# FFN of a hybrid decoder layer: squares, weight sums and sums for the residual moved between ScalarE, VectorE, GpSimd and PSUM

## The chip, the cores and the metric

The kernel runs on 1 core of one Trainium2 chip. The metric is the device time of one execution in microseconds (us); lower is better. Engines: PE is TensorE, DVE is VectorE, ACT is ScalarE, POOL is GpSimd, SP is SyncE, which issues the loads and stores of the stage in question.

## What is computed

The reference is one decoder layer: RMS norm, an RWKV-7 branch and a dilated attention branch with gates, a memory cross-attention, a squared-ReLU MLP (FFN) and a final RMS norm, on 1024 tokens of 1024 channels in fp32. The change lies in the FFN alone, which runs from 1719.5 us to the end:

```python
# D_MODEL = 1024, SEQ = 1024, FFN_DIM = 4096
u = rmsnorm(h, norm_ffn_g[l]) @ ffn_w1[l]
h = h + (jnp.square(jax.nn.relu(u)) @ ffn_w2[l]).astype(h.dtype)
return rmsnorm(h, norm_final_g)
```

## The kernel before

The FFN multiplies two by two blocks of matrices with seven block products in place of eight. There are 16 **up items** (p = 0 to 15, two 128-column tiles of `ffn_w1` each, both halves of the tokens) and then 4 **groups** of 4 **down items** (g, q: a quarter of the 4096 hidden channels, two tiles of the output). An item has seven **products** j = 0 to 6. A product (`seventh`) sums 4 blocks of 128 channels, and each block takes three matmuls of 128x512, high by high, high by low and low by high part (`L1422` to `L1424`), so it has 12 matmuls, and its sum stays in one of 4 PSUM tiles `ms`. After a product, `up_evac` or `down_evac` takes it off PSUM.

- **Weights** (`weights`): four quarters a0 to a3 (tile `sr`, 6 buffers, 256 KB each) are loaded from HBM on SP's queue. Sums c3 (`L1401`), c2 (`L1402`), c4 (`L1407`) and c6 (`L1410`) of them are formed on DVE in SBUF tiles `ws`. Each of the seven operands is split (`f_split`) into a high part `wh` (ACT, `L1384`) and a low part `wl` (POOL, `L1385`).
- **Moving operands** `com[j]`: four pairs (`ah`, `al`; for one j called `u`) for each j. The up items share one set that `first_coms` makes during the first 50 us of the stage, when the items p = 0 to 2 (the prologue) run products in the order in which it delivers them. For each group of down items `second` makes a new set of 28 pairs: the tile `ur` is read back from a DRAM scratch (`uscr`; 6 `ur` buffers), ACT casts it to `ah` (`L1534`), ACT copies `ah` to a PSUM tile `acc` (`L1536`), and DVE subtracts that from `ur` to give `al` (`L1537`). One pair in four goes without the PSUM copy (`L128`, `L129`).
- **up_evac** sums products into u11, u12, u21 and u22, squares each after ReLU with one DVE instruction (`squared`, `L1429`), forms t1 (`L1488`), t2 (`L1489`), the new u12 (`L1490`) and t4 (`L1491`) on DVE in SBUF, and stores seven tiles to `uscr`.
- **down_evac** adds the products to the residual `h` (SBUF). It keeps a running sum t (tile `sg`, SBUF). For j = 0 it is an ACT copy of the product (`L1503`), for j = 2 and j = 4 a DVE add (`sg<-sg,ms`). t is added to one h tile by DVE for j = 0, by POOL for j = 2, and to one by POOL and one by DVE for j = 4 (`h<-h,sg`). The other sums take a product straight from PSUM (`h<-h,ms`). All adds stand on `L1432`.

Products run in the order item:0, previous:5, item:1, previous:6, item:2, 3, 4, and the scheduler may interleave neighbours matmul by matmul. So a group's first item reads its new operands right after the previous item's j = 4, and 24 matmuls of previous:5 and previous:6 lie among them. The scheduler fixes each engine's order of instructions; each engine then runs strictly in that order and waits for semaphores. The pool behind `acc` has two buffers, handed out in program order: a tile of it can only be written when the tile two before it has been read for the last time. The pool behind `f` (`fps`) has two PSUM buffers too and is used by the norms at the FFN's start and end.

Of the kernel before, what the change touches and what calls it, by code (L numbers as in the profile page):

```python
# [41 lines left out]
def hybrid_layer(ctx, tc, x, mem, norm_mix_g, w_in, shift_mu, w0, w2, a0, a2, g2, k_k, k_a, r_k, gn_w, gn_b,  # L42
# [1336 lines left out]
    def f_split(raw):  # L1379
# [5 lines left out]
        nc.gpsimd.tensor_tensor(l, raw, h.bitcast(F32), op=ALU.subtract)  # L1385
# [5 lines left out]
    def weights(views, early=False):  # L1391
# [4 lines left out]
        def get(j):  # L1396
            if j < 2:
                return f_split(f_raw(views[j]) if early else a[j])
            if not c:
                c[3], c[2] = f_sum(), f_sum()  # L1400
                nc.vector.tensor_tensor(c[3], a[2], a[3], op=ALU.add)  # L1401
                nc.vector.tensor_tensor(c[2], c[3], a[0], op=ALU.subtract)  # L1402
            if j in (2, 3):
                return f_split(c[j])
            if j == 4:
                c[4] = f_sum()
                nc.vector.tensor_tensor(c[4], a[0], a[2], op=ALU.subtract)  # L1407
# [20 lines left out]
    def squared(dst, src):  # L1428
        nc.vector.scalar_tensor_tensor(dst, src, 0.0, src, op0=ALU.max, op1=ALU.mult)  # L1429

    def add(dst, a, b, eng=None):
        (eng or nc.vector).tensor_tensor(dst, a, b, op=ALU.add)  # L1432

    def up_evac(p, st, j):
# [8 lines left out]
        elif j == 1:  # L1443
            st["11"] = staged() if p >= PRO else bt.tile([P, H2], F32, tag="nt", name=nm("ua"))
            add(st["11"], st["a"], ps)
            if p >= PRO:
                squared(st["11"], st["11"])
            else:
                nc.scalar.activation(st["11"], st["11"], AF.Relu)
                nc.scalar.activation(st["11"], st["11"], AF.Square)  # L1450
# [29 lines left out]
        elif j == 6:  # L1480
# [5 lines left out]
            squared(u12, u12)  # L1486
            t1, t2, t4 = [staged() for _ in range(3)]
            nc.vector.tensor_tensor(t1, u12, u11, op=ALU.subtract)  # L1488
            nc.vector.tensor_tensor(t2, u22, t1, op=ALU.subtract)  # L1489
            nc.vector.tensor_tensor(u12, u22, u12, op=ALU.subtract)  # L1490
            nc.vector.tensor_tensor(t4, u21, t2, op=ALU.subtract)  # L1491
# [5 lines left out]
    def down_evac(g, q, st, j):  # L1497
        (h11, h12), (h21, h22) = [[hT[2 * q + e][half] for half in range(2)] for e in range(2)]
        ps = st["p", j]
        if j in (0, 2, 4):  # L1500
            t = staged()
            if j == 0:
                nc.scalar.copy(t, ps)  # L1503
            else:
                add(t, st["t"], ps)
            st["t"] = t
        if j == 0:
            add(h11, h11, t, nc.vector)
        elif j == 1:
            add(h11, h11, ps)  # L1510
        elif j == 2:
            add(h12, h12, t, nc.gpsimd)
        if j == 4:
            add(h21, h21, t, nc.gpsimd)
            add(h22, h22, t, nc.vector)
# [107 lines left out]
    def item(views, evac, **kw):  # L1623
        return dict(st={}, w=weights(views), evac=evac, **kw)

    def up_item(p):
        return item(up_views(p), lambda st, j: up_evac(p, st, j))
# [112 lines left out]
```

## Time and profile before

| | us |
|---|---|
| median of 3 runs (lowest to highest) | 2409.03 (2401.53 to 2418.07) |
| profiled execution | 2407.52 |
| its span | 2405.8 |
| PE busy in the span | 2292.9 (95%) |
| DVE / ACT / POOL busy | 1545.9 / 1088.3 / 889.4 |

The profiled execution's time is 1.7 us longer than its span. A matmul's busy time is longer than the pace at which matmuls follow each other, since they overlap; so PE's loss in a stretch is read as the stretch's length less the number of its matmuls times the undisturbed pace. In rows of the trace a line number such as L1422 is that of the kernel before, "x" counts instructions, and the last bracket gives the idle time of the engine before the row and what ended it.

### The profile page before, as it was taken

The page shows a single profiled execution, that of the slowest core. Times are in us where ns is not written, and L with a number is a line of the kernel's source. Part 1 is how long each engine was busy: PE and PEld are TensorE (multiplying, and loading weights), DVE is VectorE, ACT ScalarE, POOL GpSimd, SP SyncE. Part 2 cuts the span into 40 slices and gives each one's busy share as a digit, 9 for nine tenths or more (in the row PEclk, how much of TensorE's full clock was granted, in tenths as well). Part 3 has the DMA queues.
Part 4 walks back from the last instruction along what each step waited for, and adds up shares of the span by engine and source line. Part 5 has one row for each costly group of instructions (what it writes and reads, how often), then busy time and mean ns, then how long its engine had stood idle before and what let it go on. Part 6 is the DMA issues. An engine that isn't in the chain of part 4 may idle for free. (4 is left out here: it accounts for less than half of the span.)

```text
span 2405.8 us, 47020 instructions
## 1 busy us (share of the span) xinstructions
PE 2292.9 (95%) x18645; PEld 1827.2 (76%) x18645; DVE 1545.9 (64%) x2735; ACT 1088.3 (45%) x2118; POOL 889.4 (37%) x737
## 2 busy tenths in 40 slices
PE   6999999999999999999999999999989999899997
PEld 5777777777777777777777888888768888678785
DVE  6638676786776722233474666345799898876685
ACT  5525645546455434333443445444432222565464
POOL 4321222222222223111245534423535554566664
PEclk9999999999999999999999999999999999999998
DMA  5221111111111123121245554223244444653352
GB/s 174 58 65 35 37 39 35 37 42 28 34 38 37 46 67 106 41 67 45 82 149 161 168 150 135 81 61 87 81 133 152 149 145 160 217 167 118 119 156 71
DMA packets 301619, 226.73 MB, mean 94 GB/s; under 512 B 16229, under 2 KB 252375, under 8 KB 301399
## 3 DMA queue, kind: packets, MB, share of 16 engines
q1 hardware_dynamic: 301111, 223.20, 30.6%
q8 instruction: 147, 2.41, 0.4%
q14 instruction: 73, 0.60, 0.1%
q10 hardware_dynamic: 288, 0.52, 0.1%
HBM read 169.99 MB, written 53.67 MB: 93 GB/s over the span
## 5 line engine op out<-in xcount | busy, mean ns | idle before, releaser
L143 PE MATMUL acc<-ah,wh 128*128 128x512 f32 (+1 forms) x1600 | 652.4, 408 | 8.4 <-DVE al L1266 2.9
L144 PE MATMUL acc<-al,wh 128*128 128x512 f32 (+1 forms) x1600 | 618.2, 386 | 2.8 <-POOL al L231 1.5
L145 PE MATMUL acc<-ah,wl 128*128 128x512 f32 (+1 forms) x1600 | 618.2, 386 | 0.4 <-POOL wl L112 0.4
L112 POOL TENSOR_TENSOR wl<-wr,wh 128x512 fp32r<-128x512 f32 x248 | 334.6, 1350 | 706.9 <-ACT wh L110 668.3
L143 PEld LDWEIGHTS acc<-ah,wh 128*128 128x128 f32 x1600 | 302.8, 189 | 76.3 <-issue 3.9
L145 PEld LDWEIGHTS acc<-ah,wl 128*128 128x128 f32 x1600 | 302.7, 189 | 62.5 <-POOL wl L112 1.0
L144 PEld LDWEIGHTS acc<-al,wh 128*128 128x128 f32 x1600 | 303.4, 190 | 50.9 <-POOL al L231 3.3
L110 ACT CAST wh<-wr 128x512 fp32r<-128x512 f32 (+1 forms) x296 | 179.6, 607 | 299.2 <-PE acc L144 186.1
L1423 PE MATMUL ms<-al,wh 128*128 128x512 f32 x768 | 304.5, 396 | 10.4 <-DVE al L1537 5.4
L1422 PE MATMUL ms<-ah,wh 128*128 128x512 f32 x768 | 304.4, 397 | 5.4 <-ACT ah L128 2.5
L1424 PE MATMUL ms<-ah,wl 128*128 128x512 f32 x768 | 302.3, 394 | 0.0
L1385 POOL TENSOR_TENSOR wl<-ws,wh 128x512 fp32r<-128x512 f32 x128 | 178.6, 1398 | 177.7 <-ACT wh L1384 149.6
L1385 POOL TENSOR_TENSOR wl<-sr,wh 128x512 fp32r<-128x512 f32 x96 | 140.4, 1465 | 113.7 <-ACT wh L1384 113.6
L1423 PEld LDWEIGHTS ms<-al,wh 128*128 128x128 f32 x768 | 145.2, 189 | 48.7 <-DVE al L129 9.5
L1422 PEld LDWEIGHTS ms<-ah,wh 128*128 128x128 f32 x768 | 145.1, 189 | 41.9 <-ACT ah L128 5.0
L1424 PEld LDWEIGHTS ms<-ah,wl 128*128 128x128 f32 x768 | 145.2, 189 | 31.9 <-POOL wl L1385 0.2
L1384 ACT CAST wh<-ws 128x512 fp32r<-128x512 f32 x128 | 79.0, 620 | 171.5 <-PE ms L1423 145.9
L1384 ACT CAST wh<-sr 128x512 fp32r<-128x512 f32 x96 | 59.5, 620 | 147.7 <-PE ms L1423 136.7
L937 DVE CUSTOM_DVE_ANT_0 sS<-pS,bias 128x128 f32<-128x128 f32 (+1 forms) x96 | 30.2, 349 | 113.5 <-PE pS L125 113.3
L399 ACT ACTIVATE gt<-acc 128x512 f32<-128x512 f32 x32 | 19.0, 594 | 127.1 <-PE acc L145 121.3
L942 ACT ACTIVATE sS<-sS,nm 128x128 f32<-128x128 f32 (+1 forms) x96 | 42.5, 443 | 75.2 <-DVE nm L940 72.1
L1432 DVE TENSOR_TENSOR sg<-sg,ms 128x512 f32<-128x512 f32 x70 | 47.7, 683 | 37.5 <-PE ms L1424 36.6
(420 smaller groups left out, 4048.3 us busy)
## 6 DMA issues: line engine op xcount, KB each, us to landing
sr<-in_ffn_w_dram SPq DMA_DIRECT2D x134, 256.0 KB
wr<-in_w_in_dram SPq DMA_DIRECT2D x120, 256.0 KB
ur<-uscr SPq DMA_DIRECT2D x112, 256.0 KB
uscr<-sg SPq DMA_DIRECT2D x93, 256.0 KB
gtscr<-gt SPq DMA_DIRECT2D x32, 256.0 KB
g<-gtscr SPq DMA_DIRECT2D x32, 256.0 KB
wr<-in_p_rwkv_dram SPq DMA_DIRECT2D x32, 256.0 KB
wr<-in_w_out_dram SPq DMA_DIRECT2D x32, 256.0 KB
```

Of the source, the lines that this page charges most:

```text
L110: nc.scalar.copy(h, raw)
L112: lo_eng.tensor_tensor(l, raw, h.bitcast(F32), op=ALU.subtract)
L143: mms.append(nc.tensor.matmul(ps, h, ah, start=(k == 0), stop=False))
L144: mms.append(nc.tensor.matmul(ps, h, al, start=False, stop=False))
L145: mms.append(nc.tensor.matmul(ps, l, ah, start=False, stop=(k == len(acts) - 1)))
L942: nc.scalar.activation(sS[:, h, lo:], sS[:, h, lo:], AF.Exp, bias=nm2[:, h:h + 1], scale=0.125, accum_out=Og[:, b, 130 + h:131 + h])
L1384: nc.scalar.copy(h, raw)
L1385: nc.gpsimd.tensor_tensor(l, raw, h.bitcast(F32), op=ALU.subtract)
L1422: nc.tensor.matmul(ps, h[:, k, :], ah, start=(k == 0), stop=False)
L1423: nc.tensor.matmul(ps, h[:, k, :], al, start=False, stop=False)
L1424: nc.tensor.matmul(ps, l[:, k, :], ah, start=False, stop=(k == 3))
L1432: (eng or nc.vector).tensor_tensor(dst, a, b, op=ALU.add)
```

## The change

1. `squared` takes two ACT instructions (Relu in place, then Square) in place of one on DVE. Item p < 3 did so for u11 already.
2. In `up_evac` j = 6, the square of u12 goes to a PSUM tile b12 (`acc`), t2 is formed in a second one, b2, and ACT copies it from there to SBUF; three of the four subtractions read PSUM.
3. For up items from p = 3 and for the down items of groups 0 to 2, c3 and c2 are formed in the two `f` tiles in PSUM (named `wf`), and their low parts are split by DVE in place of POOL. c4 is a3 - c2 in place of a0 - a2 (the same value).
4. In `down_evac`, j = 0 adds the product itself to h11. For j = 2, t is formed in SBUF, ACT copies it to an `acc` tile b, and DVE adds b to h12 (POOL did). For j = 4 the sum goes to an `acc` tile b alone, and DVE adds it to h21 (POOL did) and h22.

In instructions of the whole program, DVE goes from 2670 to 2691, ACT from 1769 to 1926 and POOL from 724 to 642; PE (10971) and SP (905) keep theirs.

```diff
--- before.py
+++ after.py
@@ -1376,19 +1376,22 @@
         nc.sync.dma_start(t, ap)
         return t
 
-    def f_split(raw):
+    def f_split(raw, lo_eng=None):
         pool = wq[0] if wn[0] % 4 == 3 else wp
         wn[0] += 1
         h = pool.tile([P, 4, P], F32R, tag="wh", name=nm("wh"))
         l = pool.tile([P, 4, P], F32R, tag="wl", name=nm("wl"))
         nc.scalar.copy(h, raw)
-        nc.gpsimd.tensor_tensor(l, raw, h.bitcast(F32), op=ALU.subtract)
+        (lo_eng or nc.gpsimd).tensor_tensor(l, raw, h.bitcast(F32), op=ALU.subtract)
         return h, l
 
     def f_sum():
         return wrp[-1].tile([P, 4, P], F32, tag="wr", name=nm("ws"))
 
-    def weights(views, early=False):
+    def f_psum():
+        return fps.tile([P, 4, P], F32, tag="f", name=nm("wf"))
+
+    def weights(views, early=False, bank=False):
 
         a = [None if early else f_raw(v) for v in views]
         c = {}
@@ -1397,14 +1400,15 @@
             if j < 2:
                 return f_split(f_raw(views[j]) if early else a[j])
             if not c:
-                c[3], c[2] = f_sum(), f_sum()
+                c[3], c[2] = [f_psum() if bank else f_sum() for _ in range(2)]
                 nc.vector.tensor_tensor(c[3], a[2], a[3], op=ALU.add)
                 nc.vector.tensor_tensor(c[2], c[3], a[0], op=ALU.subtract)
             if j in (2, 3):
-                return f_split(c[j])
+                return f_split(c[j], nc.vector if bank else None)
             if j == 4:
+
                 c[4] = f_sum()
-                nc.vector.tensor_tensor(c[4], a[0], a[2], op=ALU.subtract)
+                nc.vector.tensor_tensor(c[4], a[3], c[2], op=ALU.subtract)
                 w = f_split(c[4])
                 c[6] = f_sum()
                 nc.vector.tensor_tensor(c[6], a[1], c[2], op=ALU.subtract)
@@ -1426,10 +1430,11 @@
                 yield
 
     def squared(dst, src):
-        nc.vector.scalar_tensor_tensor(dst, src, 0.0, src, op0=ALU.max, op1=ALU.mult)
-
-    def add(dst, a, b, eng=None):
-        (eng or nc.vector).tensor_tensor(dst, a, b, op=ALU.add)
+        nc.scalar.activation(src, src, AF.Relu)
+        nc.scalar.activation(dst, src, AF.Square)
+
+    def add(dst, a, b):
+        nc.vector.tensor_tensor(dst, a, b, op=ALU.add)
 
     def up_evac(p, st, j):
         def put(jj, t):
@@ -1443,11 +1448,7 @@
         elif j == 1:
             st["11"] = staged() if p >= PRO else bt.tile([P, H2], F32, tag="nt", name=nm("ua"))
             add(st["11"], st["a"], ps)
-            if p >= PRO:
-                squared(st["11"], st["11"])
-            else:
-                nc.scalar.activation(st["11"], st["11"], AF.Relu)
-                nc.scalar.activation(st["11"], st["11"], AF.Square)
+            squared(st["11"], st["11"])
             put(0, st["11"])
         elif p < PRO and j in (2, 3, 4):
 
@@ -1483,12 +1484,15 @@
                 nc.sync.dma_start(st["11"], uscr[p * 7 * P:(p * 7 + 1) * P, :])
             u11, u12, u21, u22 = st["11"], st["a"], st["21"], st["22"]
             add(u12, u12, ps)
-            squared(u12, u12)
+
+            b12, b2 = acc_tile(), acc_tile()
+            squared(b12, u12)
             t1, t2, t4 = [staged() for _ in range(3)]
-            nc.vector.tensor_tensor(t1, u12, u11, op=ALU.subtract)
-            nc.vector.tensor_tensor(t2, u22, t1, op=ALU.subtract)
-            nc.vector.tensor_tensor(u12, u22, u12, op=ALU.subtract)
-            nc.vector.tensor_tensor(t4, u21, t2, op=ALU.subtract)
+            nc.vector.tensor_tensor(t1, b12, u11, op=ALU.subtract)
+            nc.vector.tensor_tensor(u12, u22, b12, op=ALU.subtract)
+            nc.vector.tensor_tensor(b2, u22, t1, op=ALU.subtract)
+            nc.scalar.copy(t2, b2)
+            nc.vector.tensor_tensor(t4, u21, b2, op=ALU.subtract)
             put(3, t1)
             put(2, t2)
             put(4, u12)
@@ -1497,22 +1501,25 @@
     def down_evac(g, q, st, j):
         (h11, h12), (h21, h22) = [[hT[2 * q + e][half] for half in range(2)] for e in range(2)]
         ps = st["p", j]
-        if j in (0, 2, 4):
-            t = staged()
-            if j == 0:
-                nc.scalar.copy(t, ps)
-            else:
-                add(t, st["t"], ps)
-            st["t"] = t
         if j == 0:
-            add(h11, h11, t, nc.vector)
+            st["t"] = staged()
+            nc.scalar.copy(st["t"], ps)
+            add(h11, h11, ps)
         elif j == 1:
             add(h11, h11, ps)
         elif j == 2:
-            add(h12, h12, t, nc.gpsimd)
-        if j == 4:
-            add(h21, h21, t, nc.gpsimd)
-            add(h22, h22, t, nc.vector)
+
+            t = staged()
+            add(t, st["t"], ps)
+            st["t"] = t
+            b = acc_tile()
+            nc.scalar.copy(b, t)
+            add(h12, h12, b)
+        elif j == 4:
+            b = acc_tile()
+            add(b, st["t"], ps)
+            add(h21, h21, b)
+            add(h22, h22, b)
         if 3 in st["seen"] and 4 in st["seen"] and j in (3, 4):
             add(h22, h22, st["p", 3])
             add(h12, h12, st["p", 3])
@@ -1620,11 +1627,11 @@
         it["evac"](it["st"], j)
         yield
 
-    def item(views, evac, **kw):
-        return dict(st={}, w=weights(views), evac=evac, **kw)
+    def item(views, evac, bank=False, **kw):
+        return dict(st={}, w=weights(views, bank=bank), evac=evac, **kw)
 
     def up_item(p):
-        return item(up_views(p), lambda st, j: up_evac(p, st, j))
+        return item(up_views(p), lambda st, j: up_evac(p, st, j), True)
 
     PRO = 3
     early = []
@@ -1685,7 +1692,7 @@
                         gf.append(staged())
                         nc.scalar.dma_start(gf[e], norm_final_g[e * H2:(e + 1) * H2].rearrange("(o d) -> o d", o=1)
                                             .broadcast_to([P, H2]))
-                yield item(down_views(g, q), lambda st, j, g=g, q=q: down_evac(g, q, st, j), **kw), True
+                yield item(down_views(g, q), lambda st, j, g=g, q=q: down_evac(g, q, st, j), g < 3, **kw), True
 
     def stream():
         prev, ready = None, []
```

**VectorE at the last item of the prologue's first three, j = 6.** `ua`, `sg` with `ms` are sums of products; the row that PE's next product waits for is the first `sg<-ua,ms`. Before:

```order
L1432 TENSOR_TENSOR sg_19030<-sg_19030,ms_19150 128x512
L1402 TENSOR_TENSOR ws_19308<-ws_19307,sr_19247 128x512
L1429 SCALAR_TENSOR_TENSOR sg_19030<-sg_19030 128x512
L1407 TENSOR_TENSOR ws_19330<-sr_19247,sr_19251 128x512
L1488 TENSOR_TENSOR sg_19167<-sg_19030,sg_19163 128x512
L1410 TENSOR_TENSOR ws_19336<-sr_19249,ws_19308 128x512
L1489 TENSOR_TENSOR sg_19168<-sg_19061,sg_19167 128x512
L1490 TENSOR_TENSOR sg_19030<-sg_19061,sg_19030 128x512
L1491 TENSOR_TENSOR sg_19169<-ua_18785,sg_19168 128x512
L1432 TENSOR_TENSOR sg_19199<-ua_18886,ms_19186 128x512
```

After, where the add is L1437, c4 L1411 and the four subtractions L1491, L1492, L1493 and L1495:

```order
L1437 TENSOR_TENSOR sg_19030<-sg_19030,ms_19152 128x512
L1411 TENSOR_TENSOR ws_19342<-sr_19260,ws_19320 128x512
L1491 TENSOR_TENSOR sg_19172<-acc_19168,sg_19165 128x512
L1492 TENSOR_TENSOR sg_19030<-sg_19061,acc_19168 128x512
L1493 TENSOR_TENSOR acc_19169<-sg_19061,sg_19172 128x512
L1414 TENSOR_TENSOR ws_19348<-sr_19256,ws_19320 128x512
L1404 TENSOR_TENSOR wf_19495<-sr_19393,sr_19395 128x512
L1495 TENSOR_TENSOR sg_19174<-ua_18785,acc_19169 128x512
L1437 TENSOR_TENSOR sg_19205<-ua_18886,ms_19192 128x512
```

The square (`L1429`) is gone from VectorE and c2 (`L1402`) has moved ahead of the stretch; `L1491`, the first of the four subtractions, reads what ScalarE writes into `acc`, and c6 (`L1414` now) stands behind three of them.

**VectorE at the turn from group 0 to group 1.** Here `al` is a low part of the new group, `sg_22300<-` and `sg_22341<-` (before), `sg_22415<-` and `acc_22458<-` (after) are the running sums of the old group's last item for j = 2 and j = 4. Before:

```order
L1537 TENSOR_TENSOR al_22490<-ur_22497,acc_22500 128x512
L1432 TENSOR_TENSOR sg_22300<-sg_22222,ms_22287 128x512
L1537 TENSOR_TENSOR al_22492<-ur_22503,acc_22506 128x512
L1537 TENSOR_TENSOR al_22494<-ur_22509,acc_22512 128x512
L129 TENSOR_TENSOR al_22496<-ur_22515,ah_22495 128x512
L1537 TENSOR_TENSOR al_22544<-ur_22551,acc_22554 128x512
L1432 TENSOR_TENSOR sg_22341<-sg_22300,ms_22328 128x512
L1537 TENSOR_TENSOR al_22546<-ur_22557,acc_22560 128x512
L1432 TENSOR_TENSOR h_1_11297<-h_1_11297,sg_22341 128x512
L1537 TENSOR_TENSOR al_22548<-ur_22563,acc_22566 128x512
```

After:

```order
L1437 TENSOR_TENSOR sg_22415<-sg_22337,ms_22402 128x512
L1437 TENSOR_TENSOR h_1_11295<-h_1_11295,acc_22417 128x512
L1437 TENSOR_TENSOR acc_22458<-sg_22415,ms_22445 128x512
L1437 TENSOR_TENSOR h_0_11296<-h_0_11296,acc_22458 128x512
L1437 TENSOR_TENSOR h_1_11297<-h_1_11297,acc_22458 128x512
L1544 TENSOR_TENSOR al_22473<-ur_22480,acc_22483 128x512
L1437 TENSOR_TENSOR h_1_11297<-h_1_11297,ms_22424 128x512
L1437 TENSOR_TENSOR h_1_11295<-h_1_11295,ms_22424 128x512
L1544 TENSOR_TENSOR al_22475<-ur_22486,acc_22489 128x512
L1544 TENSOR_TENSOR al_22477<-ur_22492,acc_22495 128x512
```

Before, splits of the new group stand ahead of the sum for j = 2 and between it and the one for j = 4; after, the first split that goes through `acc` (and the first of all, since the others stand behind it) follows the three adds of j = 4.

**ScalarE at the same turn, after.** `wh` are weight casts, `acc_22417<-` is the copy of the running sum of j = 2, `acc_22483<-` the first copy of a new high part:

```order
L1541 CAST ah_22540<-ur_22548 128x512
L1541 CAST ah_22542<-ur_22554 128x512
L1384 CAST wh_22439<-ws_22437 128x512
L1384 CAST wh_22502<-sr_22464 128x512
L1384 CAST wh_22522<-sr_22318 128x512
L1516 COPY acc_22417<-sg_22415 128x512
L1384 CAST wh_22570<-sr_22466 128x512
L1384 CAST wh_22588<-ws_22443 128x512
L1543 COPY acc_22483<-ah_22472 128x512
```

Casts to `ah` run ahead of that copy as far as `ur` tiles are there, and no copy to `acc` does. In the new order of TensorE, counted in matmuls from the end of that j = 4, the low part of the 4th pair is first read by the 27th matmul, of the 8th by the 48th, of the 12th by the 60th, of the 16th by the 77th, of the 20th by the 90th, of the 24th by the 124th and of the 28th by the 135th.

**ScalarE at the last up item, j = 6, after.** `ua_21480` is its u12, `acc_21773` its t2 in PSUM, `ah` and `acc_21799` belong to the first down group:

```order
L1433 ACTIVATE ua_21480<-ua_21480 128x512
L1541 CAST ah_21844<-ur_21852 128x512
L1434 ACTIVATE acc_21772<-ua_21480 128x512
L1543 COPY acc_21799<-ah_21788 128x512
L1494 COPY sg_21777<-acc_21773 128x512
L1543 COPY acc_21805<-ah_21790 128x512
L1543 COPY acc_21811<-ah_21792 128x512
```

Its square and the copy of t2 stand between the copies of the first group's high parts; before, the low parts `al` of VectorE stood among the subtractions `L1488` to `L1491` of this item and were not tied to them through `acc`.

## Rows read from the trace of the kernel before

**Rows 1.** The page's head: span, busy time and share of each engine.

```profile
span 2405.8 us, 47020 instructions
PE 2292.9 (95%) x18645; PEld 1827.2 (76%) x18645; DVE 1545.9 (64%) x2735; ACT 1088.3 (45%) x2118; POOL 889.4 (37%) x737
```

**Rows 2.** Timeline of PE: start, duration, line; three matmuls on from the first row.

```profile
1731.18 0.39 PE L1422 MATMUL ms<-ah,wh 128*128 128x512 f32 x1
...
1731.86 0.39 PE L1422 MATMUL ms<-ah,wh 128*128 128x512 f32 x1
```

**Rows 3.** Windows: length; PE, PEld, DVE, ACT, POOL busy (x); clock; DMA; GB/s.

```profile
1720.00:1790.00 70.00, 58.17 (x225) 42.58 (x224) 66.30 (x99) 29.80 (x53) 23.57 (x18) 0.93 0.35 109
1900.00:1920.00 20.00, 20.00 (x88) 16.31 (x87) 18.33 (x20) 4.84 (x8) 10.45 (x8) 1.00 0.46 150
2040.00:2090.00 50.00, 41.67 (x167) 29.94 (x166) 44.74 (x65) 35.22 (x65) 23.95 (x17) 1.00 0.74 234
2140.00:2166.00 26.00, 23.86 (x102) 18.58 (x101) 21.46 (x28) 18.19 (x34) 15.30 (x12) 1.00 0.67 218
2220.00:2251.00 31.00, 28.45 (x114) 22.05 (x114) 24.98 (x34) 18.64 (x34) 18.35 (x13) 0.94 0.61 194
2300.00:2326.00 26.00, 25.36 (x111) 20.40 (x110) 23.42 (x32) 18.95 (x35) 17.53 (x13) 1.00 0.63 195
```

**Rows 4.** VectorE's instruction groups, 1715 to 2387 us: busy us, mean ns | idle before.

```profile
L1432 DVE TENSOR_TENSOR h<-h,ms 128x512 f32<-128x512 f32 x79 | 52.2, 677 | 4.4 <-PE ms L1424 4.4
L1407 DVE TENSOR_TENSOR ws<-sr,sr 128x512 f32<-128x512 f32 x32 | 47.1, 1472 | 2.4 <-POOL wl L1385 2.4
L1429 DVE SCALAR_TENSOR_TENSOR sg<-sg 128x512 f32<-128x512 f32 x45 | 45.3, 1008 | 0.9
L1432 DVE TENSOR_TENSOR h<-h,sg 128x512 f32<-128x512 f32 x32 | 34.6, 1084 | 8.3 <-ACT sg L1503 7.9
```

**Rows 5.** ScalarE's instruction groups of the same stretch.

```profile
L1536 ACT COPY acc<-ah 128x512 f32<-128x512 f32 x76 | 43.9, 586 | 7.3 <-DVE al L1537 4.3 <-issue 1.8 <-ACT ah L1534 0.3
L1534 ACT CAST ah<-ur 128x512 fp32r<-128x512 f32 x72 | 43.3, 618 | 22.0 <-DMA ur<-uscr 20.5 <-PE ms L1424 1.1
L1449 ACT ACTIVATE ua<-ua 128x512 f32<-128x512 f32 x3 | 1.9, 632 | 0.0
```

**Rows 6.** GpSimd's instruction groups of the same stretch.

```profile
L1385 POOL TENSOR_TENSOR wl<-ws,wh 128x512 fp32r<-128x512 f32 x128 | 178.6, 1398 | 177.7 <-ACT wh L1384 149.6 <-PE ms L1424 10.7 <-PE ms L1423 7.2
L1432 POOL TENSOR_TENSOR h<-h,sg 128x512 f32<-128x512 f32 x32 | 47.2, 1476 | 14.1 <-DVE sg L1432 8.8 <-PE ms L1424 5.4
```

**Rows 7.** Timeline of VectorE in the prologue, ten rows from u12's sum on.

```profile
1770.91 0.69 DVE L1432 TENSOR_TENSOR sg<-sg,ms 128x512 f32<-128x512 f32 x1 [0.18 <-PE ms L1424]
...
1773.14 1.77 DVE L1429 SCALAR_TENSOR_TENSOR sg<-sg 128x512 f32<-128x512 f32 x1
...
1780.61 0.68 DVE L1432 TENSOR_TENSOR sg<-ua,ms 128x512 f32<-128x512 f32 x1
```

**Rows 8.** Timeline of PE at the same place.

```profile
1781.43 0.47 PE L1422 MATMUL ms<-u,wh 128*128 128x512 f32 x1 [3.42 <-DVE sg L1432]
```

**Rows 9.** The splits' own work (tile ur): length, DVE busy (x), ACT busy (x), clock, DMA.

```profile
2115.00:2135.40 20.40, 10.18 (x13) 8.47 (x15) 1.00 0.53 155
2135.40:2162.00 26.60, 10.83 (x16) 8.26 (x14) 1.00 0.71 230
```

**Rows 10.** Timeline of VectorE at the turn to group 2.

```profile
2242.59 1.76 DVE L1407 TENSOR_TENSOR ws<-sr,sr 128x512 f32<-128x512 f32 x1 [1.19 <-POOL wl L1385]
2244.28 1.27 DVE L1432 TENSOR_TENSOR h<-h,ms 128x512 f32<-128x512 f32 x2
```

**Rows 11.** Timeline of GpSimd at the same place.

```profile
2242.52 1.28 POOL L1432 TENSOR_TENSOR h<-h,sg 128x512 f32<-128x512 f32 x1
```

**Rows 12.** Timeline of PE at the same place.

```profile
2245.69 0.47 PE L1422 MATMUL ms<-u,wh 128*128 128x512 f32 x1 [2.22 <-DVE h L1432]
...
2247.19 0.63 PE L1422 MATMUL ms<-u,wh 128*128 128x512 f32 x1
```

## The prediction

> **What bounds the kernel now.** I read the head of the page first, then windows along the FFN with PE's timeline beside them, then the costs of single instructions, then the places where PE waits. PE is busy for 95% of the span, so the span is PE's work plus what PE loses [rows 1]. The change leaves PE's 10971 instructions alone; only its losses can move. Three matmuls start in 1731.86 - 1731.18 = 0.68 us, 0.2275 us apart [rows 2]. A stretch of n matmuls therefore loses its length less 0.2275 n. With that the windows give, in order [rows 3]:
>
> - prologue, 1720 to 1790: 70 - 225 x 0.2275 = 18.8 us lost;
> - a steady stretch (1900 to 1920): 20 - 88 x 0.2275 = 0, with DVE at 18.3, ACT at 4.8 and POOL at 10.5 of 20 us;
> - up to down, 2040 to 2090: 50 - 167 x 0.2275 = 12.0 us lost, with DVE at 89% and the DMA engines at 0.74;
> - the three turns between groups: 26 - 102 x 0.2275 = 2.8, 31 - 114 x 0.2275 = 5.1, 26 - 111 x 0.2275 = 0.7, together 8.6 us.
>
> So some 39 us of PE time are at stake in the FFN, and no more than that can be won before its end. PE's loss is where DVE or ACT delivers an operand late; the share of busy time says nothing on that.
>
> **The steady stretch: 0.** An up item is 84 matmuls, 19.1 us. DVE loses four squares of 1008 ns [rows 4] and gets two low parts, each with one PSUM operand; the nearest row with one PSUM operand is `h<-h,ms`, 677 ns, and above it POOL's price of 1398 ns bounds it [rows 4, 6]. DVE comes down by 4.0 - 1.4 = 2.6 us. ACT gets four pairs of Relu (632 ns) and Square, for which I take the same, and a copy of 586 [rows 5], 5.6 us: from 4.8 to about 10.5 of 20. POOL gives up 2 x 1.4 = 2.8 us. No engine passes PE's 19.1, and PE waits for none of them in this stretch already; the cover is the distance between a product and its use. If that cover were gone, the price would be the longer square alone, 1.26 - 1.01 = 0.25 us x 4 an item, 13 items: 13 us. I see nothing that takes it away and count 0. c4 in its new form has one operand in PSUM: between 677 and 1472 ns [rows 4], not on PE's path here.
>
> A rule of the Trainium skill speaks against the squares: "ScalarE: Activation LUTs", Rules for kernel authors, wants relu, max and mul on VectorE, not on ScalarE. The rows agree on the sign (1008 ns against twice 632), but the engine that gets the longer work is idle for three quarters of this stretch, so by the rule the sum would move only where PE waits for ACT.
>
> **Prologue: -1.5 (bounds -6 to +2).** The largest wait is 3.42 us [rows 8], and it ends with DVE's `sg<-ua,ms` of 1780.61, ten instructions behind u12's sum of 1770.91 [rows 7]. Among them are c2, which now stands ahead, and the square of 1.77 us. On the other side ACT's Relu and Square, 1.26 us, must now come before the first subtraction, with only c4 beside them. Walked by hand from 1771.6: c4 hidden, square done 1773.0, three subtractions at 0.68 to 0.9, c6, one c3, the last subtraction, and the sum starts at about 1778.3 in place of 1780.6. That is 2.3 us, and a little of the half-clock matmuls behind the wait. Against it, earlier in the prologue ACT now also squares u22 of the first item, and in its new order that stands ahead of casts to `ah`: two instructions of 0.63 us [rows 5], of which I count 0.8 as lost (up to 1.8 with the half-clock matmuls). Net -1.5; the lower end is all of the 3.42 and its slow matmuls, the upper end the squares with no gain.
>
> **Up to down: -1 (-4 to +6).** 28 splits are made here, and 28 at each turn. Here item 15's squares leave DVE, which is at 89%, and that is worth up to three squares, 3 us. But its b12 and b2 now take both `acc` buffers in the middle of the first group's splits: the next split's copy waits for the four subtractions, and ACT stands with it. Before, splits were mixed with those subtractions. Walking the new order with the durations of [rows 4, 5], PE waits some 5 to 6 us for the first product after item 15's chain, 3 for the next that reads new splits, and 2 after that: 10 to 12 us in place of 12.0. The price if it goes wrong is one wait for a whole chain of squares and subtractions, 1.3 + 3 x 0.7 + 0.6 = 4 us, and a half more for the copy of t in the group's first item behind it.
>
> **Turns between groups: +8.5 (-5 to +38).** This is the term that decides. Before, DVE had made 13 of the new group's splits in the 20 us ahead of the running sum of j = 4 (2135.4), and 16 in the 26.6 us after it [rows 9]; together 1.62 us a split, unhurried. After, the copy of j = 2's t and the sum of j = 4 take both `acc` buffers, and 21 of 28 splits need `acc`; in DVE's new order the first of all stands behind the adds of j = 4. So nothing is ready when that product ends. PE has 24 matmuls of the old item to fill in (5.5 us).
>
> Let the first split end 2.6 us later (the sum, two adds and one subtraction of some 0.65 each) and each further one r us after the last: the n-th ends at 2.6 + (n - 1) r. It is due at the matmul that first reads it: the 12th at 60 x 0.2275 = 13.6, the 16th at 17.5, the 20th at 20.5, the 28th at 30.7. What is r? ACT has 21 copies of 586 ns and some 22 casts of 618 left after the sum (six `ur` tiles can be cast before), 25.9 us [rows 5], and about eight weight casts and copies, 5 us: 31 us, 1.1 a split. DMA has 22 loads of 0.262 MB and 1.5 items of weights, 7.3 MB at 234 GB/s [rows 3]: 31 us as well. DVE has 28 low parts and some 14 sums with a PSUM operand at 677 ns [rows 4], 28 us, and the weight sums. Three engines in a ring that has two buffers will not run at their own best at once; above stands 1.62 of before. I take 1.2, nearer to the sums, since before the splits had the time and were not asked for faster. Then the 12th ends 2.1 us late (15.8), the 20th 4.9 (25.4), the 28th 4.3 (35.0). PE's waits add up to the latest of these, 4.9 us a turn, and I add 0.8 for the copy of the new item's own j = 2, which stands ahead of later casts on ACT: 5.7, three times 17.
>
> What goes away: 8.6, with the waits for POOL. At the turn to group 2 the 2.22 us wait and the half-clock matmuls behind it (0.63 us long) [rows 12] follow from DVE's c4, which waited 1.19 for POOL's low part and took 1.76, and two h adds behind it [rows 10], while POOL did an h add of 1.28 [rows 11]. These holds of 1 to 1.5 us are gone. 17 - 8.6 = +8.5. Lower bound: r = 1.0, where only the 20th is late (1.1): 3 in all for the three turns, -5. Upper: r = 1.62, the 28th 15.6 late, 47 - 8.6 = +38.
>
> **End of the FFN: 0 (-1 to +1).** In group 3 no weight sum sits in PSUM; the two POOL adds of 1476 ns an item become DVE adds of 677 [rows 4, 6], one ACT copy lies between, and PE does not wait there.
>
> **Sum.** 0 - 1.5 - 1 + 8.5 + 0 = +6 against the profiled execution's own 2407.5 (span 2405.8 and 1.7 around it): **2413.5**. That execution lies 1.5 us below the median of the three runs, whose spread is 17 us, so I don't correct for it. Some 1% (24 us: below 2385 or above 2433) is about what a measurement of this kernel tells from no change.
>
> **Rivals.**
> - *The forecast: turns get somewhat longer, little else moves.* 2403 to 2427. Chance 0.55.
> - *Relief wins (faster).* DVE's adds with two SBUF operands take 1084 ns, with one in PSUM 677, and c4 1472 [rows 4], and c4 waits and swells beside POOL's work [rows 10, 11]; if much of DVE's queue is swollen by POOL, removing POOL's adds and DVE's squares pays at every wait. Prologue -6, up to down -4, turns -5: 2407.5 - 15 = 2392.5. It decides if r is at most 1.0. Against it: the acc ring, which no faster DVE unties. Chance 0.18, of which 0.06 below 2385, where two thirds of all the loss would have to go. The Trainium skill has a rule for it: "SBUF — State Buffer", Who interferes with whom, lets a DVE instruction with two SBUF operands and a GpSimd one that reads SBUF shut each other out, and not one with a PSUM operand; the two durations of the h add agree.
> - *All hidden.* The change moves work between engines that PE does not wait for, and the turns keep 13 splits' worth of slack by DVE's saved time: 2407.5 with 5 on either side. This lies within 1%; for it speaks the steady stretch, against it the order at the turns. Chance 0.12.
> - *Splits run at the old pace (slower).* If after the sum the splits run at 1.62 us, as over the whole of a turn before [rows 9], then each turn loses 15.6 us: 2407.5 - 2.5 + 38 = 2443. With DMA at 0.67 to 0.74 in these stretches [rows 3] and ACT behind each load, that can be; it decides from r = 1.47, where the 28th is 11.6 late and three turns reach +26. Long waits also bring half-clock matmuls as in [rows 12]. Chance 0.15, 0.12 of it above 2433.
>
> **The numbers.** Faster by over 1%: 0.06. Slower by over 1%: 0.12. Within: 0.82. The range, 2394 to 2435, leaves out about two thirds of the relief case and two thirds of the slow one, 0.2. The likeliest case has 2403 to 2427.
>
> **What would show it.** In windows of the steady stretch of after: 88 matmuls in 20 us, ACT near 10, DVE near 15, POOL near 7.5. In the prologue the wait of 3.42 near 1. At each turn, no `al` of the new group before the running sum of j = 4, then waits of PE on `al` and `ah` of 1 to 3 us each, some 5 to 6 a turn, and no wait for POOL. It would be wrong if splits appear ahead of that sum, if their pace after it is 1.0 or 1.6, or if PE waits in the steady stretch for a square.

## The result and the profile after

The changed kernel takes **2426.92 us** (median of 7 runs, 2423.44 to 2434.64) against 2403.83 for the kernel before (7 runs, 2401.53 to 2418.07): a ratio of 1.0084, 95% interval 1.0067 to 1.0101. It is 0.84% slower, some 20 us (23 between the medians). That lies inside the range given, and it is three to four times the 6 us that were forecast; the sign of the sum was right and its size was not.

The head of the page, span and engines, after:

```profile
span 2424.9 us, 47039 instructions
PE 2300.2 (95%) x18645; PEld 1830.7 (75%) x18645; DVE 1462.9 (60%) x2756; ACT 1181.9 (49%) x2272; POOL 756.9 (31%) x655
```

Beside [rows 1], VectorE has 83 us less to do, GpSimd 133 us less and ScalarE 94 us more, and the span is 19.1 us longer. Work moved as the diff says; none of these sums tells the time. The windows do (length; PE, PEld, DVE, ACT, POOL busy; granted clock; DMA share; GB/s); the first three answer to [rows 3], the others are the three turns with their ends:

```profile
1720.00:1790.00 70.00, 60.04 (x234) 43.77 (x233) 61.33 (x95) 37.57 (x66) 24.37 (x19) 0.93 0.36 113
1900.00:1920.00 20.00, 20.00 (x88) 16.27 (x88) 10.99 (x17) 10.86 (x19) 7.61 (x6) 1.00 0.44 150
2040.00:2090.00 50.00, 40.47 (x157) 30.96 (x156) 38.15 (x60) 37.23 (x69) 10.32 (x8) 0.90 0.71 226
2130.00:2180.00 50.00, 45.75 (x187) 35.29 (x186) 40.29 (x63) 34.40 (x63) 13.20 (x11) 0.97 0.61 183
2215.00:2262.00 47.00, 42.51 (x179) 32.48 (x178) 38.65 (x61) 33.70 (x62) 11.56 (x10) 1.00 0.62 191
2300.00:2345.00 45.00, 39.07 (x156) 29.76 (x155) 33.61 (x51) 32.41 (x67) 16.28 (x12) 0.92 0.58 176
```

The steady stretch holds 88 matmuls in 20 us as before, with ScalarE at 10.9, VectorE at 11.0 and GpSimd at 7.6. Up to down loses 50 - 157 x 0.2275 = 14.3 us, the first turn 50 - 187 x 0.2275 = 7.5, the second 47 - 179 x 0.2275 = 6.3. (The third has transposes among its matmuls, so there the gaps between starts are summed.) In the same way, by gaps over 0.2275 us, this table gives PE's loss in each stage for every kernel of the study; "FFN" is the time from its first to its last 128x512 matmul. These are profiles of one execution each, and where the FFN begins differs between them by up to 11 us for the same code ahead of it, so the FFN's own length is the thing to compare.

| kernel | FFN | prologue | up to down | three turns | ratio to before (interval) |
|---|---|---|---|---|---|
| before | 667.2 | 19.2 | 12.2 | 8.2 | 1 |
| changed | 684.4 | 17.5 | 14.3 | 22.4 | 1.0084 (1.0067 to 1.0101) |
| part 4 alone | 686.9 | 17.6 | 14.7 | 26.0 | 1.0099 (1.0084 to 1.0114) |
| part 4 alone, tiles from f | 660.4 | 19.1 | 10.3 | 3.2 | 0.9974 (0.9955 to 0.9993) |
| changed, j = 2 in SBUF | 680.1 | 17.4 | 13.4 | 20.7 | 1.0072 (1.0055 to 1.0089) |
| changed, j = 4 in SBUF | 672.8 | 16.1 | 14.2 | 14.9 | 1.0040 (1.0024 to 1.0057) |
| changed, both in SBUF | 666.0 | 17.5 | 13.7 | 7.3 | 1.0001 (0.9984 to 1.0018) |
| changed without part 4 | 658.2 | 17.6 | 13.5 | 0.0 | 0.9975 (0.9962 to 0.9988) |
| parts 1 and 3, sums in SBUF on VectorE | 661.3 | 17.5 | 8.0 | 8.4 | 0.9967 (0.9952 to 0.9982) |
| part 1 alone | 659.1 | 13.9 | 11.9 | 5.7 | 0.9984 (0.9963 to 1.0006) |
| parts 1 and 2, tiles from f | 659.8 | 13.9 | 11.6 | 6.5 | 0.9972 (0.9955 to 0.9988) |
| part 3 alone | 655.4 | 22.8 | 5.2 | 0.0 | 0.9974 (0.9956 to 0.9991) |
| parts 1 and 3 | 649.7 | 17.4 | 5.1 | 0.0 | 0.9945 (0.9928 to 0.9963) |
| parts 1 and 3, old c4 in the prologue | 649.0 | 13.9 | 8.1 | 0.0 | 0.9936 (0.9919 to 0.9953) |

Two of the rows need care: in "part 4 alone, tiles from f" and "changed, j = 4 in SBUF" the turns hold a wait of the final norm's transposes (2.5 and 1.6 us) that is counted apart for the changed kernel, and the second of them is the profile of its fastest execution, 6 us under its median.

Between the two kernels the FFN grew by 17.2 us: prologue -1.7, up to down +2.1, turns +14.2, one wait near the end (for the final norm's transposes) +1.8, and 0.8 in small gaps. The split work (tile ur) around the first turn, in 20.4 us ahead of the running sum of j = 4 and 26.6 us behind it (VectorE, ScalarE, clock, DMA):

```profile
2116.70:2137.10 20.40, 0.00 (x0) 3.75 (x6) 1.00 0.18 52
2137.10:2163.70 26.60, 13.93 (x20) 9.29 (x16) 0.94 0.69 207
```

Beside [rows 9], 13 splits ahead of the sum have become none. ScalarE made its six casts, as many as there are ur tiles, and stopped. The longest wait of that turn on PE, and what the chain of waits (start, duration, what) holds just ahead of it:

```profile
2155.57 0.74 PE L1426 MATMUL ms<-ah,wh 128*128 128x512 f32 x2 [3.08 <-ACT ah L1541]
...
2157.05 0.63 PE L1426 MATMUL ms<-ah,wh 128*128 128x512 f32 x1
```

```profile
2149.33 0.61 DVE al L1544
2149.95 2.84 DMA ur<-uscr
2152.82 0.62 ACT ah L128
2153.44 0.52 ACT wh L1384
2153.96 0.49 ACT acc L1516
2154.44 0.52 ACT acc L1543
2154.96 0.56 ACT ah L1541
```

A split ends on VectorE and so frees an `ur` tile; its load takes 2.84 us; ScalarE stands for that load; and the cast that PE needs is queued behind the load's own cast, a weight cast, the copy `L1516` of the new item's running sum and the first copy to acc. PE stands for 3.08 us and then runs more than 3 us at half clock, matmuls of 0.63 us (granted clock 0.50 from 2156.7 to 2159.5, the level of 1.2 GHz). VectorE's splits pause at the same time:

```profile
2150.44 0.69 DVE L129 TENSOR_TENSOR al<-ur,ah 128x512 fp32r<-128x512 f32 x1
...
2154.48 0.69 DVE L1437 TENSOR_TENSOR h<-h,acc 128x512 f32<-128x512 f32 x1
2155.08 0.68 DVE L1544 TENSOR_TENSOR al<-ur,acc 128x512 fp32r<-128x512 f32 x1
```

The twelfth split ends at 2151.13, 14.0 us after the running sum of j = 4 began (2137.08), and the thirteenth starts at 2155.08. VectorE is not idle in between: it makes a weight's low part, three weight sums, the new item's running sum and the h add that the copy `L1516` feeds. The second turn's wait has the same chain, with a load of 2.76:

```profile
2240.15 0.73 PE L1426 MATMUL ms<-ah,wh 128*128 128x512 f32 x2 [2.82 <-ACT ah L1541]
```

At the third, 4.55 us, something else is late ahead of the same copy, a weight sum that waited for GpSimd:

```profile
2319.85 1.71 POOL wl L1385
2321.55 0.02 issue
2321.57 1.73 DVE ws L1404
2323.31 0.61 DVE sg L1437
2323.92 0.02 issue
2323.94 0.59 ACT acc L1516
2324.53 0.52 ACT acc L1543
2325.05 0.56 ACT ah L1541
```

### The profile page after: what moved, and what is told of

Its sections match the earlier page's. It is cut to its first block, busy times and chain, and to the rows that moved or that the text cites. A ratio compares the mean times of both kernels' runs of the same rounds, so it can differ in the third digit from the quotient of the medians.

```text
span 2424.9 us, 47039 instructions
## 1 busy us (share of the span) xinstructions
PE 2300.2 (95%) x18645; PEld 1830.7 (75%) x18645; DVE 1462.9 (60%) x2756; ACT 1181.9 (49%) x2272; POOL 756.9 (31%) x655
## 5 line engine op out<-in xcount | busy, mean ns | idle before, releaser
L1427 PE MATMUL ms<-al,wh 128*128 128x512 f32 x768 | 305.8, 400 | 11.2 <-DVE al L1544 9.5
L1385 POOL TENSOR_TENSOR wl<-sr,wh 128x512 fp32r<-128x512 f32 x96 | 129.2, 1350 | 187.0 <-ACT wh L1384 176.5
L1385 POOL TENSOR_TENSOR wl<-ws,wh 128x512 fp32r<-128x512 f32 x78 | 103.3, 1326 | 263.0 <-ACT wh L1384 254.0
L1384 ACT CAST wh<-ws 128x512 fp32r<-128x512 f32 x78 | 48.4, 622 | 93.3 <-PE ms L1427 73.7
L1437 DVE TENSOR_TENSOR h<-h,ms 128x512 f32<-128x512 f32 x96 | 63.6, 684 | 19.5 <-PE ms L1428 18.6
```

The source lines that it names most:

```text
L1384: nc.scalar.copy(h, raw)
L1385: (lo_eng or nc.gpsimd).tensor_tensor(l, raw, h.bitcast(F32), op=ALU.subtract)
L1427: nc.tensor.matmul(ps, h[:, k, :], al, start=False, stop=False)
L1437: nc.vector.tensor_tensor(dst, a, b, op=ALU.add)
```

## The experiments

**Which part: without part 4.** The edit puts the old `down_evac` back:

```diff
-            b = acc_tile()
-            nc.scalar.copy(b, t)
-            add(h12, h12, b)
+            add(h12, h12, t, nc.gpsimd)
...
-            b = acc_tile()
-            add(b, st["t"], ps)
-            add(h21, h21, b)
-            add(h22, h22, b)
+            add(h21, h21, t, nc.gpsimd)
+            add(h22, h22, t, nc.vector)
```

> The change without its part 4: down_evac as in the kernel before (t in SBUF, GpSimd's two adds), the rest as changed. Theory A (the two acc buffers tie the next group's splits to the old item's sums): splits stand ahead of the running sum of j = 4 again, the turns lose about 8 us in place of 22, and the time is 13 to 15 us below the changed kernel, about 2412. Theory B (ScalarE's added work, most of it squares and weight handling, makes the casts late): the turns keep 18 to 22 us and the time stays at 2423 to 2427.

Measured 2399.07 us (before 2407.91 on the same chip), the FFN 26.2 us shorter than in the changed kernel. The turns do not go back to before's 8 us; they go to nothing: at the first one 219 matmuls stand in 50 us with PE busy for all of them.

```profile
2130.00:2180.00 50.00, 50.00 (x219) 40.80 (x218) 40.04 (x60) 31.57 (x58) 28.92 (x21) 1.00 0.62 193
```

So parts 1 to 3 remove the waits of before at the turns, and part 4 alone makes all of those of after. Theory B falls: ScalarE has the squares here too.

**Part 4 alone**, put into the kernel before.

> The kernel before with part 4 alone. Theory A: the turns lose 20 to 22 us without any square or weight sum moved, and the time is 12 to 15 us above before. Theory B: within 5 us of before.

2428.47 against 2407.91, 0.99% slower: the whole of the loss, with no square and no weight sum moved. Its longest wait at the first turn is again for a cast, and longer; in its chain a weight load of 4.32 us is what comes late ahead of the same copy:

```profile
2155.32 1.22 PE L1422 MATMUL ms<-ah,wh 128*128 128x512 f32 x2 [4.43 <-ACT ah L1537]
```

**The pool or the work: part 4 alone, with b from the f pool.**

```diff
-            b = acc_tile()
+            b = fps.tile([P, H2], F32, tag="f", name=nm("b"))
```

(twice). The copy on ScalarE, the adds on VectorE and the bytes are those of the run above; only the buffers are others.

> The kernel before with part 4 alone, as in the run of part 4 alone (0.99% slower), but its PSUM tiles b come from the f pool, which the down items do not use here, and not from acc. ScalarE's copy and VectorE's adds are the same. Theory A (the two acc buffers): splits stand ahead of the sum of j = 4 again, the turns lose under 10 us and the time is within 6 us of before, or below it since GpSimd's adds are gone: 2396 to 2412. Rival D (the copy on ScalarE in the middle of the casts, or the adds on VectorE, not the pool): turns keep 20 us or more and the time is 15 us or more above before.

2399.68 against 2405.66, 0.26% faster than before, and 26.5 us of FFN less than with acc. The split work around the sum of j = 4 (which starts at 2132.38 here) is that of [rows 9] again, 13 splits ahead of it:

```profile
2112.00:2132.40 20.40, 8.47 (x13) 8.28 (x14) 1.00 0.58 180
2132.40:2159.00 26.60, 10.55 (x16) 8.37 (x14) 1.00 0.72 222
```

and the turns hold nearly the full pace (217 x 0.2275 = 49.4 of 50 us in the first, PE busy for 49.74):

```profile
2125.00:2175.00 50.00, 49.74 (x217) 40.26 (x216) 40.14 (x62) 32.02 (x59) 24.76 (x19) 1.00 0.57 174
2210.00:2260.00 50.00, 49.91 (x218) 40.43 (x217) 41.03 (x59) 26.67 (x49) 24.37 (x18) 1.00 0.51 156
```

This settles it. What made the change slower is that two sums went into a pool of two buffers whose tiles are handed out in program order, and that the splits of the next group take their tiles from the same pool. Rival D, the copy or the adds themselves, falls.

**Which of the two tiles: j = 2 from SBUF, and j = 4 from SBUF.** In the first, `add(h12, h12, t)` on VectorE stands for the copy and its tile; in the second, t of j = 4 is an SBUF tile and VectorE adds it twice.

> The changed kernel with h12's add of j = 2 from SBUF on VectorE (no ScalarE copy, no acc tile there); j = 4 keeps its sum in acc. It tells the two uses of acc apart. If the copy behind which casts wait (the 3 to 4.5 us waits of TensorE on casts) is most of the loss, turns fall to 8 to 12 us, 2410 to 2415; if it is the tile of j = 4, ahead of which no split is made, they stay at 18 to 22, 2422 to 2427.

2423.69, turns 20.7: the tile of j = 4 is enough to hold the splits, and the copy behind which casts wait is not most of the loss. The pause between the twelfth and the thirteenth split shrinks from 4.0 to 0.8 us at the first turn, and the turns lose nearly as much. The wait has moved. Without the copy, the casts go ahead, and PE waits for a weight's low part on VectorE that is queued behind the late splits:

```profile
2159.55 0.51 PE L1428 MATMUL ms<-ah,wl 128*128 128x512 f32 x1 [3.10 <-DVE wl L1385]
```

> The changed kernel with j = 4's sum in an SBUF tile, VectorE adding it to h21 and h22; j = 2 keeps its ScalarE copy to acc. Its counterpart, with j = 4 in acc alone, kept the turns at 20.7 us of 22.4. If either use of acc is enough to hold the splits, the turns stay at 12 us or more here too, 2415 to 2425; if only the tile of j = 4 holds them, they fall to 6 or 8 us, as with both sums in SBUF, 2405 to 2410.

2418.78, turns 14.9, of which 1.6 is the wait near the end: the tile of j = 2 is enough for more than half of it. Either use holds the ring; they are not to be summed.

**Both sums in SBUF, on VectorE.**

```diff
-            b = acc_tile()
-            nc.scalar.copy(b, t)
-            add(h12, h12, b)
+            add(h12, h12, t)
...
-            b = acc_tile()
-            add(b, st["t"], ps)
-            add(h21, h21, b)
-            add(h22, h22, b)
+            t = staged()
+            add(t, st["t"], ps)
+            add(h21, h21, t)
+            add(h22, h22, t)
```

> The change with part 4's sums kept in SBUF tiles and added to h by VectorE: no acc tile and no ScalarE copy in down_evac, and nothing on GpSimd. Theory A: as without part 4, turns near 8 us, about 2412; if GpSimd's adds cost something of their own, 3 to 5 us less than that, 2407 to 2409. Theory B: 2420 to 2427. Rival C (VectorE's adds with two SBUF operands are what costs): slower than the run without part 4 by 3 us or more.

2405.60, level with before, and 6.5 us above the run that leaves `down_evac` as it was, the time that rival C asked for. With part 3 in, GpSimd has room for its two adds an item, and with them on VectorE the turns lose 7.3 us where they lost none (h11's sum straight from PSUM is the only other difference; how the adds bring it about was not looked into, so rival C's reason, their two SBUF operands, is not shown). Taking GpSimd's two adds off it does not pay here even without acc.

**Parts 1 and 3 with the same SBUF sums (u12 and t2 as before).**

> Parts 1 and 3 only (squares on ScalarE, c3 and c2 in PSUM with their low parts on VectorE), with part 4's sums in SBUF on VectorE and u12 and t2 in SBUF as before: no use of acc but for the splits. Theory A: up to down also falls to 12 us or less, turns to 8 or less; the time is 0 to 6 us below before, 2398 to 2404. Theory B: 5 us or more above before.

2399.43, at the low end; up to down falls from 13.7 to 8.0 as part 2 goes, and the turns stay at 8.4.

**Parts 1 and 3 alone.** Old `down_evac`, and u12 and t2 in SBUF.

> Parts 1 and 3 with down_evac and u12 and t2 as before. Theory A: turns at 0 as in the run without part 4, up to down near 8 us as in the run with neither, so some 5 us below the run without part 4: 2392 to 2396, the fastest. Rival E (what u12 and t2 cost at up to down hangs on SBUF sums on VectorE): up to down stays near 13 us, 2399.

2391.76 against 2405.66, 0.55% faster. Up to down, then the turns:

```profile
2040.00:2090.00 50.00, 45.87 (x197) 36.13 (x196) 44.38 (x64) 34.84 (x66) 22.47 (x17) 1.00 0.75 240
2130.00:2180.00 50.00, 50.00 (x219) 40.79 (x218) 37.30 (x57) 23.44 (x43) 24.67 (x18) 1.00 0.46 139
2215.00:2262.00 47.00, 47.00 (x206) 38.34 (x205) 30.91 (x46) 18.40 (x33) 27.72 (x20) 1.00 0.41 125
```

50 - 197 x 0.2275 = 5.2 us lost at up to down against 13.5 with part 2: part 2 costs 8.4 us there. Rival E falls.

**Part 3 alone.** As above, with the squares back on VectorE.

> Part 3 alone: c3 and c2 in PSUM, their low parts on VectorE, c4 from c2; squares on VectorE. If taking the splits off GpSimd is what empties the turns, turns lose 0 to 2 us and the time is 6 to 9 us below before, 2396 to 2400. If the squares on ScalarE did it, turns stay near 8 us and the time at before's. VectorE is fuller at up to down, 10 to 14 us there.

2400.05 against 2405.66. The turns are empty: it was the weight sums, not the squares. Up to down is 5.2, where 10 to 14 was expected, so a fuller VectorE (48.5 us of 50) did no harm there. Of the loss at up to down and the turns in before, 20.4 us, part 3 alone takes away 15.2; in the prologue it loses 22.8 in place of 19.2.

**Part 1 alone.**

> Part 1 alone: every square as Relu and Square on ScalarE, all else as before. From the two runs of part 3 with and without it: the prologue loses 5 us less, the turns stay at about 8 us, up to down stays at 8 to 12: 3 to 8 us below before. If ScalarE's longer square is a cost of its own (1.26 against 1.0 us), PE waits in the steady stretch and the time is before's or up to 13 us above.

2404.59 against 2407.76, a ratio of 0.9984 whose interval reaches over 1: the time does not tell. In the trace the prologue loses 13.9 in place of 19.2, and nothing is lost in the steady stretch.

**Parts 1 and 2, with b12 and b2 from f.**

```diff
-            b12, b2 = acc_tile(), acc_tile()
+            b12, b2 = [fps.tile([P, H2], F32, tag="f", name=nm("b")) for _ in range(2)]
```

> Part 1 and part 2, with b12 and b2 from the f pool (part 3 is out, so it is free) and not from acc. Part 2 with acc costs 8.4 us at up to down (13.5 with it, 5.1 without). Theory A (the acc buffers again): here it costs nothing against part 1 alone, within 3 us of it at up to down. Rival F (the copy of t2 on ScalarE and its wait): up to down 5 us or more above part 1 alone.

Up to down loses 11.6 against 11.9 with part 1 alone: the detour of u12 and t2 over PSUM and ScalarE costs nothing when it is not in acc. It is the same ring once more.

**A faster version.** Parts 1 and 3, with c4 = a0 - a2 where the sums are in SBUF.

```diff
-                nc.vector.tensor_tensor(c[4], a[3], c[2], op=ALU.subtract)
+                nc.vector.tensor_tensor(c[4], *((a[3], c[2]) if bank else (a[0], a[2])), op=ALU.subtract)
```

> Parts 1 and 3 as in their own run (0.55% faster), but c4 is a0 - a2 again for the prologue's weights and a3 - c2 only where c2 lies in PSUM; so the prologue's weight sums stand in VectorE's order as they do with part 1 alone, which lost 13.9 us there against 17.4. If that form of c4 is what costs there, the prologue loses about 14, up to down 5, the turns 0, and the time is 17 us below before, 2386 to 2391. If not, the time is that of parts 1 and 3, 2389 to 2394.

2389.43 against 2406.04, 0.64% faster (interval 0.9919 to 0.9953). The prologue lost 13.9 as expected, but up to down 8.1 where 5 was expected, for no reason that I found; the FFN is as long as without the edit within 0.7 us, and the two intervals overlap. Parts 1 and 3 are the better kernel; the last edit is not shown to add to it.

## Why the prediction was wrong

**Steady stretch: 0, right.** 88 matmuls in 20 us, with ScalarE at 10.9 (forecast 10.5). VectorE came down further than the forecast (11.0, not 15), since more than the squares got cheaper. These are VectorE's and ScalarE's groups of the changed kernel in the FFN (busy, mean ns):

```profile
L1385 DVE TENSOR_TENSOR wl<-wf,wh 128x512 fp32r<-128x512 f32 x50 | 34.0, 686 | 16.1 <-ACT wh L1384 16.1
L1437 DVE TENSOR_TENSOR h<-h,acc 128x512 f32<-128x512 f32 x48 | 31.5, 684 | 6.8 <-ACT acc L1516 6.2
L1493 DVE TENSOR_TENSOR acc<-sg,sg 128x512 f32<-128x512 f32 x16 | 20.5, 1280 | 0.0
L1411 DVE TENSOR_TENSOR ws<-sr,wf 128x512 f32<-128x512 f32 x25 | 17.0, 680 | 0.0
```

With an operand in PSUM the h add takes 684 ns (1084 with two in SBUF [rows 4]), c4 680 (1472), and the low part 686 where GpSimd took 1398 [rows 6]; the one subtraction that still reads two SBUF tiles, `L1493`, takes 1280. It is not the second SBUF operand by itself that costs: in before, the 9 c4 that no GpSimd instruction overlaps in time take 680 ns and the other 23 take 1782; in after, the one `L1493` without such an overlap takes 695 and the other 15 take 1319, and the h add takes 683 without and 684 with one. The Trainium skill's "SBUF — State Buffer", Who interferes with whom, where a VectorE instruction with two SBUF inputs contends with a GpSimd one that reads SBUF and one with at most one does not, is borne out by these. The lower bound of 677 was about the price of every instruction with a PSUM operand.

**Prologue: -1.5, measured -1.7, the right number by luck.** The wait of 3.42 us [rows 8] is gone, but not because the sum that PE waited for comes 2.3 us earlier: it comes at 1781.90, 0.6 us earlier than before when both are counted from the FFN's first matmul (1721.44 and 1719.51), and PE had other products until then. Nor did ScalarE's squares earlier in the prologue eat the gain: the squares alone give -5.3 there (13.9), with no such cost. What takes 3.5 of that back is c4 = a3 - c2 (17.4 with parts 1 and 3, 13.9 with the old c4 in the prologue), which the prediction counted at nothing.

**Up to down: -1, measured +2.1.** Both terms were mis-sized. The relief was put at up to 3 us for the squares off VectorE; the squares alone give 0.3 (12.2 to 11.9), and part 3 alone, from which nothing was expected here, gives 7.0 (12.2 to 5.2). The acc tiles of u12 and t2 were put at about 2 on top; they cost 8.4. The hold itself is as described, in the changed kernel's ScalarE:

```profile
2061.02 0.59 ACT L1434 ACTIVATE acc<-ua 128x512 f32<-128x512 f32 x1
2062.96 0.59 ACT L1543 COPY acc<-ah 128x512 f32<-128x512 f32 x1 [1.35 <-DVE ua L1492]
2063.57 0.59 ACT L1494 COPY sg<-acc 128x512 f32<-128x512 f32 x1
```

The first copy of the new group waits for the subtraction that lets b12 go, and PE ([2.37 <-DVE al L1544] at 2064.33) for the split behind it.

**Turns: +8.5, measured +14.2. This is the step that failed.** What goes away is 8.2 us of before, as forecast (8.6), and the runs show that parts 1 to 3 take all of it, with part 3 alone enough. In before, c4 waited for GpSimd's low part to free a tile [rows 10]; with c3 and c2 in PSUM no such wait is left. What comes was put at 17 us and is 22.4. The prediction had the order right, with no split ahead of the sum of j = 4. Its price followed the low parts on VectorE, one every r us, and set each against the matmul that first reads it. **PE's waits came on another path: they end with casts on ScalarE, for high parts.** At each turn the longest one stands before the 62nd matmul behind the old item's j = 4 (2155.57, 2240.15, 2325.66). In TensorE's order this is the first to read the high part of the 17th pair, due after 62 x 0.2275 = 14.1 us; the list of due times had low parts only, and none between the 60th and the 77th matmul. At the first turn that cast ended at 2155.53, 18.4 us after the sum began. From the split that frees a `ur` tile (2149.94) to the end of that cast the chain above takes 5.6 us: a load of 2.84 and 2.7 of ScalarE's queue. No term held such a delay, since loads and casts stood in the sum as rates.

Up to and with the 62nd matmul the turns lose 4.6, 4.5 and 5.9 us, 15.0 in all. That this is close to 17 is luck, since other operands are waited for. The rest stood in the sum at nothing: half-clock matmuls behind two of the three long waits, 1.6 and 2.4 us, and smaller waits after them, some 3.5. The pace r = 1.2 was too high for the splits ahead of the long wait: the first twelve took 2151.13 - 2137.08 = 14.0 us, 1.04 us each after the first 2.6. Over all 28 it was too low, 1.30, 1.26 and 1.44 us at the three turns, but the later splits stand behind sums that wait for PE, so how much of that is the ring's own pace stays open. The term that failed is not the 0.8 us for the copy of the new item's own j = 2: the copy takes 0.49 us of the chain at the first two turns, and at the third it holds the casts while it waits for a late sum, but the run without it still loses 20.7 us, with other waits in its place. With nothing split ahead, whatever comes late (a load at two turns, a weight sum at the third) stops the casts behind it, the splits behind them and the loads into the tiles that these would free, all at once. With 13 splits of head start the same copy, loads and casts lose 0.7 us over the three turns, and 2.5 in the wait near the end, as the run with f shows.

**End of the FFN: 0, measured +1.8.** One wait of PE for `L1657` at 2354, behind a weight sum that waited 1.19 us for GpSimd and the h add after it.

**The base.** The sum stood on a profiled execution of 2407.5; the median of before over seven runs is 2403.83. Of the 23 us between the medians the traces show 19.1, of which 17.2 lie in the FFN. Against the +6 of the sum that is 11.2 too many: 5.7 at the turns, 3.1 at up to down, 1.8 near the end and 0.8 in small gaps, less 0.2 in the prologue.

**The rivals.** "Splits run at the old pace" (2443) lies 16 us above the measured time, the forecast 13 below it, and the pace was 1.04 for the first twelve splits and 1.26 to 1.44 for all 28, not 1.62. "Relief wins" (2392.5) is near the time of parts 1 and 3, which leave GpSimd its adds, and wrong about the change. "All hidden" falls with the head start at the turns. The Trainium skill's rule against relu and max on ScalarE ("ScalarE: Activation LUTs", Rules for kernel authors) agrees with the durations (633 and 634 ns against 1008) and is not borne out here as a matter of time: with part 1 alone nothing is lost in the steady stretch, the prologue loses 5.3 us less and the ratio is 0.9984, not told from 1.

## What to carry to other kernels

A buffer pool with two buffers, handed out in program order, ties everything that uses it together. Before a tile is put there, list who takes the next two tiles and on which engines those stand. Here moving an operand to PSUM made single instructions up to twice as fast (c4 1472 to 680 ns); with the sums of part 4 in acc the kernel was slower by 0.99%, and with the same sums in another pool it was faster by 0.26%.

When an order leaves a queue no head start, do not price it as a pace plus small delays: list for every operand, high parts as well as low parts, the matmul that first reads it, then what stands ahead of that operand in its engine's queue, and what each of those can wait for. And split a change of four parts before believing in its sum: here two parts win 0.55% and the other two lose 1.4%.

## What the runs showed of the hardware

Two waits of nearly the same length differ in what follows: behind the 3.08 us of the first turn come matmuls of 0.63 us (granted clock 0.50 from 2156.7 to 2159.5, the level of 1.2 GHz), behind 2.82 us at the second none do (1.00, the level of 2.4 GHz). ScalarE's write to PSUM is no dearer than to SBUF: 603 ns for the square into acc (`L1434`, 13 instructions), 634 into SBUF.
